# Plain float32 products for the last three down tiles, a final norm without GpSimd, and first low parts from VectorE

## The chip, the cores and the metric

The kernel runs on one core of a Trainium2 chip. The metric is the device time of one execution in microseconds, lower is better. Of the engines, PE is TensorE (matrix products), DVE is VectorE, ACT is ScalarE, POOL is GpSimd and SP is SyncE, which here only issues DMAs.

## The reference, cut to what matters

One encoder layer on 1024 rows of width 1024: attention, mLSTM and a gated MLP side by side, a layer norm, then a mixture of 16 experts in which each expert chooses 128 rows, and a last layer norm. Only the part from the experts on is touched.

```python
def expert_choice_ffn(h, w_router, w_gate, w_up, w_down):
    cap = max(1, min(S, EC_CAPACITY_FACTOR * S // N_EXPERTS))      # 128 rows an expert
    aff = softmax(einsum('bsd,de->bse', h, w_router))
    gate, idx = lax.top_k(aff.transpose(0, 2, 1), cap)
    xg = jax.vmap(lambda hb, ib: hb[ib])(h, idx)
    hid = silu(einsum('becd,edf->becf', xg, w_gate)) * einsum('becd,edf->becf', xg, w_up)
    ye = einsum('becf,efd->becd', hid, w_down) * gate[..., None]
    ...                                                             # scatter-add of ye to the rows

    y = expert_choice_ffn(h2, w_router, w_gate, w_up, w_down)
    return layer_norm(DN_ALPHA * x + (1 + g2) * y, ln_g[1], ln_b[1])
```

Everything is float32; D is 1024, the hidden width F is 2048.

## The kernel before

**Splitting.** PE multiplies float32 here in three products of a shorter format, fp32r: an operand is split in a high part H (ACT copies it to fp32r) and a low part L (the operand minus H, by DVE or POOL), and `mm3` (lines 42 to 44) adds H by H, H by L and L by H. `split` (lines 37 and 38) does it for activations, `part` (lines 1295 and 1296) for weights.

**Tiles.** `experts` walks the weights in 192 tiles of 2 MB, four quarters of F an expert: gate tile g n, up tile u n, and down tile d n-1 for n from 0 to 63. `fetch` loads a tile on SP's queue into one of eight raw buffers, as soon as the four parts of the tile that held it are made. Each tile has four pieces of 128x1024; `part` makes H and L of a piece, in a ring of NP = 5 pairs, five pieces ahead of `product`, which issues six products of 128x512 for it (two column halves, three products each). Down products of an expert add up in one accumulator `ye` of 128x1024 in PSUM.

**An expert's rows.** `pick` (lines 1303 to 1318) makes a one-hot matrix on DVE, multiplies it on PE to the list of chosen rows `ix` and their gates `sw`, and gathers the rows by an indirect DMA on POOL (line 1315) to `xg`; `turn` transposes them on PE and splits them (`xH`, `xL`). `gate` is the silu on ACT, `hidden` the product with the up result on DVE, `turn_hidden` (T, line 1376) the transposes and `parts_hidden` (U) the split of the hidden rows. `finish` scales an expert's result and adds it to the rows in DRAM (`acc_dr`) by an indirect DMA on POOL; all rows there already hold the residual.

**Start.** Ahead of the experts lies `routing`, the choice of rows: a sort on DVE whose steps are the maximum and minimum at lines 1201 and 1202. `experts` is written behind it: eight fetches, the first five parts with their L on POOL, then `pick(0)` and `turn(0)`.

**End.** The order of the last 16 products and of the final norm is written out in the string `LAST`. Each word is an operation with a number: P product, W part, T and U as above, G and H the last `gate` and `hidden`, L row loads to three raw buffers, Q the gather of the last expert's rows from `acc_dr`, y and z that expert's scaled result plus those rows, and then for rows i (eight tiles of 128 rows, and tile 8 for the last expert's 128 chosen rows) the sums by ACT (a) or DVE (d), the root (q), the reciprocal (r), the normalisation (p by ACT), the gain (g by POOL, m by DVE), the shift (s by POOL, h by DVE), or gain and shift in two fused steps on DVE (e, f). Z scatters tile 8 over the output by an indirect DMA on POOL, behind the writes of all others. An engine works off its instructions in the order of this string.

Of the kernel before, what the change touches and what calls it, by code (L numbers as in the profile page):

```python
# [25 lines left out]
class K:  # L26
# [1233 lines left out]
    def experts(self):  # L1260
        nc, tc, a, v, s, g, pe = self.nc, self.tc, self.a, self.v, self.s, self.g, self.pe
        NR, NP = 8, 5
        with tc.tile_pool(name="ew", bufs=1, reuse_waits="tile") as ew, \
# [26 lines left out]
            def part(eng):  # L1290
                t, q = divmod(len(pieces), 4)
                H = ew.tile([128, 1024], F32R, tag="wH", name=f"H{t}_{q}", bufs=NP)
# [92 lines left out]
            for i in range(NP):  # L1385
                part(g)
            for f in (pick, turn):
                for _ in f(0):
                    pass
            nc.scalar.dma_start(g2r, self.bcast_rows(self.mod_dr[3:4, :], 1024))  # L1390
            all_ = 4 * len(tiles)
            for i in range(all_ - 16):
# [161 lines left out]
```

## Time and profile before

| | us |
|---|---|
| median of 3 runs | 1718.21 (1717.98 to 1719.55) |
| the profiled execution | 1719.36 |
| its span, first to last instruction | 1717.6 |
| PE busy in the span | 1590.0 (93%) |
| DVE busy | 1498.6 (87%) |
| ACT busy | 1124.4 (65%) |
| POOL busy | 300.8 (18%) |
| mean granted clock of TensorE | 0.965 |

The shares are means over stages with different limits, so they are read stage by stage: the attention part and routing to 573.57 us, the experts from there to 1648.81 (the start of the last but one hidden tile's transposes, T0), the last 16 pieces to the end of PE at 1676.27, and the rest of the final norm to 1717.57.

### The profile page before, as it was taken

How to read it: one execution, taken by the hardware profiler on the slowest of the kernel's cores; microseconds unless marked ns; L12 is line 12 of the kernel's file. 1: busy time of each engine (PE TensorE's matmuls, PEld its weight loads, DVE VectorE, ACT ScalarE, POOL GpSimd, SP SyncE). 2: the span in 40 equal slices, each digit the busy share in tenths (PEclk: the TensorE clock that was granted, in tenths of full speed). 3: DMA queues.
4: the chain of work that ended last, by engine and by line, in shares of the span. 5: the costliest groups of instructions: out<-in, count | busy, mean ns of one | idle time of the engine just before them, and what ended most of it. 6: DMA issues, size and time to landing. Idle time of an engine off the chain costs nothing.

```text
span 1717.6 us, 22528 instructions
## 1 busy us (share of the span) xinstructions
PE 1590.0 (93%) x8147; PEld 1338.3 (78%) x8147; DVE 1498.6 (87%) x2031; ACT 1124.4 (65%) x1446; POOL 300.8 (18%) x338
## 2 busy tenths in 40 slices
PE   5889999999993799999999999999999999999990
PEld 5678799798883588888888888888888888888870
DVE  6878863597987699999999999999999999999987
ACT  4443433496222478787878787778787878787873
POOL 2514331285115000000000000000000000000045
PEclk9899999999995799999999999999999999999995
DMA  9154631113369499999999999999999999999933
GB/s 341 63 173 154 212 103 31 62 50 113 114 256 341 140 387 380 386 386 376 388 382 379 391 383 388 385 377 389 384 378 390 382 387 385 378 386 386 368 134 121
DMA packets 218823, 498.33 MB, mean 290 GB/s; under 512 B 9420, under 2 KB 31784, under 8 KB 218712
## 3 DMA queue, kind: packets, MB, share of 16 engines
q1 hardware_dynamic: 209680, 467.77, 73.9%
q0 software_dynamic: 5984, 21.60, 4.5%
q10 hardware_dynamic: 3048, 7.52, 1.2%
q8 instruction: 64, 1.05, 0.3%
q14 instruction: 47, 0.39, 0.1%
HBM read 475.79 MB, written 21.07 MB: 289 GB/s over the span
## 4 chain that ended last, share of the span: by engine, by line
PE 83%; DVE 12%; issue 2%; ACT 1%; DMA 1%; POOL 1%; ACTq 0%; SPq 0%; POOLq 0%; DVEq 0%
PE pu L42 7%; PE pg L42 7%; PE pg L44 7%; PE pg L43 7%; PE pu L44 7%; PE pu L43 7%; PE ye L42 7%; PE ye L44 7%; PE ye L43 7%; PE mx L44 2%; PE mx L42 2%; PE mx L43 2%; PE ht L1376 2%; PE tp L42 2%; PE tp L43 1%
## 5 line engine op out<-in xcount | busy, mean ns | idle before, releaser
L1296 DVE TENSOR_TENSOR L<-rd,H 128x1024 fp32r<-128x1024 f32 x251 | 306.5, 1243 | 27.2 <-ACT H L1295 21.4
L1296 DVE TENSOR_TENSOR L<-ru,H 128x1024 fp32r<-128x1024 f32 x253 | 306.5, 1229 | 23.3 <-ACT H L1295 12.8
L1295 ACT ACTIVATE H<-ru 128x1024 fp32r<-128x1024 f32 x256 | 271.9, 1063 | 83.4 <-PE pg L44 61.9
L1295 ACT ACTIVATE H<-rd 128x1024 fp32r<-128x1024 f32 x256 | 271.0, 1059 | 73.8 <-PE pg L44 47.3
L1295 ACT ACTIVATE H<-rg 128x1024 fp32r<-128x1024 f32 x256 | 271.6, 1062 | 63.4 <-PE ye L44 54.6
L1296 DVE TENSOR_TENSOR L<-rg,H 128x1024 fp32r<-128x1024 f32 x252 | 302.3, 1220 | 7.5 <-ACT H L1295 1.6
L42 PE MATMUL pg<-H,xH 128*128 128x512 f32 x512 | 207.4, 405 | 0.0
L44 PE MATMUL pg<-H,xL 128*128 128x512 f32 x512 | 201.1, 393 | 0.0
L42 PE MATMUL pu<-H,xH 128*128 128x512 f32 x512 | 200.6, 392 | 0.0
L43 PE MATMUL pg<-L,xH 128*128 128x512 f32 x512 | 200.5, 392 | 0.0
L44 PE MATMUL pu<-H,xL 128*128 128x512 f32 x512 | 199.2, 389 | 0.0
L43 PE MATMUL pu<-L,xH 128*128 128x512 f32 x512 | 199.2, 389 | 0.0
L43 PE MATMUL ye<-L,hH_h 128*128 128x512 f32 x504 | 196.5, 390 | 1.8 <-POOL L L1296 1.8
L42 PE MATMUL ye<-H,hH_h 128*128 128x512 f32 x504 | 197.6, 392 | 0.0
L44 PE MATMUL ye<-H,hL_h 128*128 128x512 f32 x504 | 196.3, 389 | 0.0
L1315 POOL DMA_INDIRECT xg<-h_dr,ix x16 | 23.9, 1491 | 848.8 <-PE ye L44 724.8
L44 PEld LDWEIGHTS pg<-H,xL 128*128 128x128 f32 x512 | 96.5, 188 | 21.0 <-DVE xL L38 0.2
L44 PEld LDWEIGHTS pu<-H,xL 128*128 128x128 f32 x512 | 96.1, 188 | 20.2
L43 PEld LDWEIGHTS ye<-L,hH_h 128*128 128x128 f32 x504 | 94.7, 188 | 21.8 <-POOL L L1296 2.6
L43 PEld LDWEIGHTS pu<-L,xH 128*128 128x128 f32 x512 | 96.1, 188 | 19.6
L42 PEld LDWEIGHTS pu<-H,xH 128*128 128x128 f32 x512 | 96.1, 188 | 19.6
L43 PEld LDWEIGHTS pg<-L,xH 128*128 128x128 f32 x512 | 97.0, 189 | 17.6
(453 smaller groups left out, 3040.5 us busy)
## 6 DMA issues: line engine op xcount, KB each, us to landing
rg<-in_w_gate_dram SPq DMA_DIRECT2D x64, 2048.0 KB, 9.1
ru<-in_w_up_dram SPq DMA_DIRECT2D x63, 2048.0 KB, 11.8
rd<-in_w_down_dram SPq DMA_DIRECT2D x63, 2048.0 KB, 11.0
B<-in_w_ada_dram SPq DMA_DIRECT2D x64, 256.0 KB, 3.0
B<-in_w_in_dram SPq DMA_DIRECT2D x18, 512.0 KB, 4.9
H<-in_w_ada_dram SPq DMA_DIRECT2D x8, 1024.0 KB, 10.9
B<-in_x_dram SPq DMA_DIRECT2D x4, 1024.0 KB, 5.5
B<-in_w_out_dram SPq DMA_DIRECT2D x8, 512.0 KB, 3.2
```

What stands on the lines that cost most here:

```text
L42: pe.matmul(out, sH, mH, start=first, stop=False)
L43: pe.matmul(out, sH, mL, start=False, stop=False)
L44: pe.matmul(out, sL, mH, start=False, stop=last)
L1295: s.activation(H, src, AF.Copy)
L1296: eng.tensor_tensor(L, src, H.bitcast(F32), ALU.subtract)
L1315: g.indirect_dma_start(out=xg, out_offset=None, in_=self.h2_dr, in_offset=bass.IndirectOffsetOnAxis(ap=ix[:, :1], axis=0))
L1376: pe.transpose(p[:, k, :], state["sg"][:, 128 * k:128 * k + 128], self.idn)
```

## The change

It has five parts.

1. At the start, `pick(0)` comes first; then four parts, with L on DVE; then `turn(0)`; then the fifth part, with L on DVE.
2. The last three down tiles, d61 to d63, are not split: `part` hands out the raw piece, `product` issues two plain float32 products for it in place of six, and the hidden rows of these tiles are one float32 copy by ACT.
3. The fetches of d62 and d63 are taken out of `part` and placed in `LAST` (F) behind the row loads L0, L1 and L2; Q comes directly behind them.
4. In the final norm POOL does nothing but the two indirect DMAs. Row sums are made by ACT (a) or, for row 1 and tile 8, by DVE; then two fused steps on DVE, e: (x - mean) * gain and f: times the reciprocal, plus shift.
5. The last tile's products are ordered by column halves, A12 to A15 for the first half and B12 to B15 for the second, and y, z and the statistics x of tile 8 are steps of half a row.

```diff
+            plain = lambda t: tiles[t][0] == "d" and tiles[t][1] >= 4 * NE - 3
...
             def part(eng):
                 t, q = divmod(len(pieces), 4)
+                if plain(t):
+                    pieces.append((raws[t][:, 1024 * q:1024 * q + 1024], None))
+                    return
...
-                if q == 3 and len(raws) < len(tiles):
+                if q == 3 and len(raws) < len(tiles) - 2:
                     fetch(nc.sync)
...
-            def product(i):
+            def product(i, us=(0, 1)):
...
-                    for u in range(2):
+                    H, L = hid[n]
+                    for u in us:
                         c = slice(512 * u, 512 * u + 512)
+                        if L is None:
+                            pe.matmul(state["acc"][:, c], H[:, q, :], WH[:, c], start=(j + q == 0), stop=(j == 3 and q == 3))
+                            continue
...
+            def parts_hidden(n):
+                if n >= 4 * NE - 3:
+                    H = ew.tile([128, 4, 128], F32, tag=("hH", "hL", "xH")[n - 4 * NE + 3], name=f"h{n}", bufs=1 + (n == 4 * NE - 1))
+                    s.activation(H, state["ht"], AF.Copy)
+                    hid[n] = (H, None)
+                    return
...
-            for i in range(NP):
-                part(g)
-            for f in (pick, turn):
-                for _ in f(0):
-                    pass
+
+            for _ in pick(0):
+                pass
+            for i in range(NP - 1):
+                part(v)
+            for _ in turn(0):
+                pass
+            part(v)
...
+        def sums(i):
             m, x = mv[:, i, :], X[i]
+            s.activation(B[11], x, AF.Identity, accum_out=m[:, 3:4])
+            s.activation(m[:, 0:1], m[:, 3:4], AF.Copy, scale=-1.0 / D)
+            s.activation(B[11], x, AF.Square, bias=m[:, 0:1], accum_out=m[:, 1:2])
...
+        def gain(i):
+            v.scalar_tensor_tensor(X[i], X[i], mv[:, i, 0:1], B[0], op0=ALU.add if byact[i] else ALU.subtract, op1=ALU.mult)
+
+        def shift(i):
+            v.scalar_tensor_tensor(X[i], X[i], mv[:, i, 2:3], B[1], op0=ALU.mult, op1=ALU.add)
             if i < 8:
                 nc.sync.dma_start(a["out"][0, 128 * i:128 * i + 128, :], X[i])
...
+        def scaled(q):
+            c = slice(512 * q, 512 * q + 512)
+            v.scalar_tensor_tensor(X[8][:, c], state["acc"][:, c], state["w"][:, 2:3], g2r[:, c], op0=ALU.mult, op1=ALU.mult)
+
+        def final_sum(q):
+            c = slice(512 * q, 512 * q + 512)
+            v.tensor_tensor(X[8][:, c], X[8][:, c], B[10][:, c], ALU.add)
+
+        def spread(q):
+            v.bn_stats(st8[:, q, :], X[8][:, 512 * q:512 * q + 512])
+            if q:
+                v.bn_aggr(mv[:, 8, 0:2], st8)
...
-    LAST = "T0 P0 P1 P2 W0 W1 W1 P3 U0 P4 W0 G0 P5 P6 W1 L0 L1 P7 W1 L2 W1 H0 W0 P8 P9 W0 W0 T1 U1 W1 P10 P11 P12 P13 d0 d1 W1 P14 q0 r0 q1 d2 r1 d3 p0 P15 p1 a5 y8 d4 q4 d6 Q0 g0 r4 q5 g1 q6 d7 s0 p4 q3 r5 p5 q7 r6 z8 r3 h1 q2 m5 g4 p3 s4 p6 r7 m3 m6 s5 r2 h6 e7 s3 f7 p2 a8 q8 r8 g2 h2 p8 m8 s8 Z0"
+    LAST = "L0 L1 F0 L2 F0 Q0 T0 U0 W0 a0 d1 P0 P1 e0 e1 a2 W0 e2 W0 P2 W0 P3 G0 q0 q1 q2 r0 f0 r1 f1 r2 f2 P4 P5 P6 P7 H0 a3 e3 q3 r3 f3 a4 e4 q4 r4 f4 W0 W0 W0 W0 W0 W0 W0 W0 P8 P9 T1 U1 P10 P11 a5 e5 q5 r5 f5 A12 A13 A14 A15 B12 B13 B14 B15 a6 e6 a7 y0 z0 x0 q6 r6 f6 e7 q7 r7 f7 y1 z1 x1 q8 e8 r8 f8 Z0"
```

How the change moves the instructions shows at three places. The first is DVE's end of the routing and start of the experts; OH and ix are `pick(0)`, xL is `turn(0)`, and L_0 to L_3 are low parts of weight pieces (rg, ru: raw gate and up tile). Before:

```order
L1303 TENSOR_TENSOR OH_5246<-C,late 128x1024 [waits DVE_49]
L1311 COPY sw_5257<-sp_5248 128x6 [waits PE_49]
L1313 TENSOR_TENSOR ix_5259<-sw_5257 128x1 [waits DVE_49]
L1317 TENSOR_TENSOR sw_5257<-sw_5257 128x1
L1318 TENSOR_TENSOR sw_5257<-sw_5257 128x1 [waits DVE_49]
L38 TENSOR_TENSOR xL_5266<-xt_5267,xH_5265 128x512 [waits DMAHW5_49,DMASW2_49,Activation_49]
L38 TENSOR_TENSOR xL_5266<-xt_5274,xH_5265 128x512 [waits Activation_49]
L1296 TENSOR_TENSOR L_1_5290<-ru_5210,H_1_5289 128x1024 [waits DMAHW1_49,Activation_49]
```

And with the change:

```order
L1308 TENSOR_TENSOR OH_5224<-C,late 128x1024 [waits DVE_49]
L1316 COPY sw_5235<-sp_5226 128x6 [waits PE_49]
L1318 TENSOR_TENSOR ix_5237<-sw_5235 128x1 [waits DVE_49]
L1322 TENSOR_TENSOR sw_5235<-sw_5235 128x1
L1323 TENSOR_TENSOR sw_5235<-sw_5235 128x1 [waits DVE_49]
L1301 TENSOR_TENSOR L_0_5244<-rg_5208,H_0_5243 128x1024 [waits DMAHW7_49,Activation_49]
L1301 TENSOR_TENSOR L_1_5248<-rg_5208,H_1_5247 128x1024 [waits Activation_49]
L1301 TENSOR_TENSOR L_2_5252<-rg_5208,H_2_5251 128x1024 [waits Activation_49]
L1301 TENSOR_TENSOR L_3_5256<-rg_5208,H_3_5255 128x1024 [waits Activation_49]
L38 TENSOR_TENSOR xL_5262<-xt_5263,xH_5261 128x512 [waits DMAHW5_49,DMASW2_49,Activation_49]
L38 TENSOR_TENSOR xL_5262<-xt_5270,xH_5261 128x512 [waits Activation_49]
L1301 TENSOR_TENSOR L_0_5278<-ru_5210,H_0_5277 128x1024 [waits DMAHW1_49,Activation_49]
```

The four low parts of the first gate tile and the first of the up tile now stand in DVE's row, around the pair of xL; before, POOL had them ahead of its gather.

The second place is ACT's row at the last gate and up tiles, from the last up tile's first high part (H_0<-ru) on; hH_h and h are copies of the hidden rows, fx the accumulated rows, fmv their statistics. Before:

```order
L1295 ACTIVATE H_0_14648<-ru_14298 128x1024 [waits DMAHW4_49,DVE_49,PE_49]
L1295 ACTIVATE H_1_14652<-ru_14298 128x1024 [waits DVE_49,PE_49]
L1295 ACTIVATE H_2_14656<-ru_14298 128x1024 [waits DVE_49,PE_49]
L37 ACTIVATE hH_h_14666<-ht_14624 128x512
L1295 ACTIVATE H_3_14677<-ru_14298 128x1024 [waits DVE_49,PE_49]
L1367 ACTIVATE sg_14681<-pg_14629 128x512 [waits PE_49]
```

And with the change:

```order
L1388 ACTIVATE h_14611<-ht_14606 128x512 [waits PE_49]
L1300 ACTIVATE H_0_14613<-ru_14298 128x1024 [waits DMAHW4_49,DVE_49]
L1473 ACTIVATE fx_14599,fmv<-fx_14587 128x1024 [waits DMAHW7_49]
L1474 ACTIVATE fmv<-fmv 128x1 [waits Activation_49]
L1475 ACTIVATE fx_14599,fmv<-fx_14587,fmv 128x1024 [waits Activation_49]
L1473 ACTIVATE fx_14599,fmv<-fx_14592 128x1024 [waits DMAHW1_49,Activation_49]
L1474 ACTIVATE fmv<-fmv 128x1 [waits Activation_49]
L1475 ACTIVATE fx_14599,fmv<-fx_14592,fmv 128x1024 [waits Activation_49]
L1300 ACTIVATE H_1_14642<-ru_14298 128x1024 [waits DVE_49,PE_49]
L1300 ACTIVATE H_2_14647<-ru_14298 128x1024 [waits DVE_49,PE_49]
L1300 ACTIVATE H_3_14657<-ru_14298 128x1024 [waits DVE_49,PE_49]
L1374 ACTIVATE sg_14667<-pg_14624 128x512 [waits PE_49]
```

Between H_0 and H_1 of the last up tile now stand the sums of two rows, and H_1 to H_3 follow them.

The third place is the end of DVE's row; fy is tile 8, L1494 (before) and L1501 the scaling of the accumulator ye. Before:

```order
L1478 TENSOR_TENSOR fx_14719<-fx_14719,fx_14699 128x1024 [waits Activation_49]
L1465 RECIPROCAL fmv<-fmv 128x1
L1469 SCALAR_TENSOR_TENSOR fmv<-fmv 128x1 [waits DVE_49]
L1484 TENSOR_TENSOR fx_14719<-fx_14719,fx_14699 128x1024
L1497 SCALAR_TENSOR_TENSOR fx_14719<-fx_14719,fmv,fx_14699 128x1024
L1482 SCALAR_TENSOR_TENSOR fx_14719<-fx_14719,fmv,fx_14699 128x1024 [waits DVE_49]
L1465 RECIPROCAL fmv<-fmv 128x1 [waits Activation_49]
L1467 TENSOR_TENSOR fmv<-fmv 128x1 [waits DVE_49]
L1484 TENSOR_TENSOR fx_14704<-fx_14704,fx_14699 128x1024 [waits Pool_49]
L1478 TENSOR_TENSOR fy<-fy,fx_14699 128x1024 [waits Activation_49]
```

And with the change:

```order
L1501 SCALAR_TENSOR_TENSOR fy<-ye_14447,sw_13712,g2r 128x512 [waits DMASW1_49,PE_49]
L1505 TENSOR_TENSOR fy<-fy,fx_14599 128x512 [waits DMASW2_49,DVE_49]
L1508 BN_STATS fst_14586<-fy 128x6 [waits DVE_49]
L1482 RECIPROCAL fmv<-fmv 128x1 [waits Activation_49]
L1489 SCALAR_TENSOR_TENSOR fx_14599<-fx_14599,fmv,fx_14587 128x1024 [waits DVE_49]
L1486 SCALAR_TENSOR_TENSOR fx_14599<-fx_14599,fmv,fx_14587 128x1024 [waits DMAHW7_49]
L1482 RECIPROCAL fmv<-fmv 128x1 [waits Activation_49]
L1489 SCALAR_TENSOR_TENSOR fx_14599<-fx_14599,fmv,fx_14587 128x1024 [waits DVE_49]
L1501 SCALAR_TENSOR_TENSOR fy<-ye_14447,sw_13712,g2r 128x512
L1505 TENSOR_TENSOR fy<-fy,fx_14599 128x512 [waits DVE_49]
L1508 BN_STATS fst_14586<-fy 128x6 [waits DVE_49]
L1510 BN_AGGR fmv<-fst_14586 128x2 [waits DVE_49]
```

Behind these follow the gain, reciprocal and shift of tile 8. The scaling of ye stands near the end now, in two halves, of which the first names a wait for PE and the second none.

## Rows read from the trace of the kernel before

**Rows 1.** the stages, table by windows; x: instructions
```profile
core 0: us, PE busy (x) PEld busy (x) DVE busy (x) ACT busy (x) POOL busy (x), PEclk, DMA share, GB/s
...
540.66:552.41 11.75, 0.00 (x0) 0.00 (x0) 11.64 (x6) 0.00 (x0) 11.63 (x6) 0.50 1.03 388
...
573.57:1648.81 1075.24, 1075.03 (x5008) 888.17 (x5009) 1014.49 (x997) 857.78 (x909) 57.49 (x30) 1.00 1.02 378
1648.81:1676.27 27.46, 23.89 (x106) 18.51 (x103) 22.05 (x23) 17.00 (x19) 22.14 (x9) 1.00 0.07 19
1676.27:1717.57 41.30, 0.00 (x1) 0.00 (x0) 32.02 (x38) 15.17 (x24) 22.88 (x10) 0.53 0.29 115
```

**Rows 2.** DVE's timeline around the routing's end and the start of the experts: start, us, what
```profile
543.22 2.26 DVE L1201 TENSOR_TENSOR T<-TB 128x64 f32<-128x64 f32 x1
...
552.41 0.23 DVE L1201 TENSOR_TENSOR T<-TB 128x64 f32<-128x64 f32 x1
...
553.60 0.23 DVE L1201 TENSOR_TENSOR TB<-T 128x64 f32<-128x64 f32 x1
...
575.40 1.50 DVE L38 TENSOR_TENSOR xL<-xt,xH 128x512 fp32r<-128x512 f32 x2 [6.80 <-ACT xH L37]
...
602.93 2.36 DVE L1296 TENSOR_TENSOR L<-rg,H 128x1024 fp32r<-128x1024 f32 x2
```

**Rows 3.** POOL's timeline over the same stretch
```profile
540.77 9.23 POOL L1296 TENSOR_TENSOR L<-rg,H 128x1024 fp32r<-128x1024 f32 x4
549.96 2.34 POOL L1296 TENSOR_TENSOR L<-ru,H 128x1024 fp32r<-128x1024 f32 x1
569.18 1.09 POOL L1315 DMA_INDIRECT xg<-h_dr,ix  x1 [16.89 <-issue]
603.51 1.48 POOL L1315 DMA_INDIRECT xg<-h_dr,ix  x1 [33.24 <-PE ye L44]
```

**Rows 4.** PE's timeline where plain float32 products stand among split ones
```profile
316.05 1.88 PE L632 MATMUL sd<-B,WT 128*128 128x512 f32 x4
317.36 0.79 PE L42 MATMUL tp<-H,B 128*128 128x512 f32 x1
318.00 0.39 PE L43 MATMUL tp<-H,B 128*128 128x512 f32 x1
```

**Rows 5.** the chain that ended last, by time, around the first products
```profile
579.20 0.43 PE pg L44
...
580.17 0.23 PE pg L44
```

**Rows 6.** the same chain, transposes of the last but one hidden tile
```profile
1649.04 0.44 PE ht L1376 x4
```

**Rows 7.** PE's timeline in the last products, two of its waits
```profile
1665.94 0.50 PE L43 MATMUL ye<-L,hH_h 128*128 128x512 f32 x1 [1.21 <-POOL L L1296]
...
1670.97 0.50 PE L44 MATMUL ye<-H,xL_h 128*128 128x512 f32 x1 [1.75 <-DVE xL_h L38]
```

**Rows 8.** ACT's timeline at the end: one high part, first and last of a row's sums
```profile
1657.77 1.06 ACT L1295 ACTIVATE H<-rd 128x1024 fp32r<-128x1024 f32 x1 [0.29 <-PE pu L44]
...
1678.89 1.04 ACT L1450 ACTIVATE fx<-fx 128x1024 f32<-128x1024 f32 x1
...
1681.34 0.19 ACT L1452 ACTIVATION_READ_ACCUMULATOR fx<-fx,fmv 128x1 f32 x1
```

**Rows 9.** SP's queue timeline, the loads of the accumulated rows
```profile
1630.57 8.94 SPq L1438 DMA_DIRECT2D fx<-acc_dr  x8
```

**Rows 10.** DVE's timeline, a fused step on half a row and on a whole row
```profile
526.26 0.75 DVE L1077 SCALAR_TENSOR_TENSOR H<-H,mm,B 128x512 f32<-128x512 f32 x1
...
1701.52 1.27 DVE L1497 SCALAR_TENSOR_TENSOR fx<-fx,fmv,fx 128x1024 f32<-128x1024 f32 x1
```

**Rows 11.** POOL's timeline, its last two
```profile
1708.95 2.34 POOL L1484 TENSOR_TENSOR fy<-fy,fx 128x1024 f32<-128x1024 f32 x1 [3.96 <-DVE fy L1478]
1711.57 1.00 POOL L1503 DMA_INDIRECT out_dram<-fy,ix  x1 [0.28 <-POOL fy L1484]
```

More of the change, by code (lines that the diff above doesn't have):

```diff
@@ L1417, in experts @@
             ops = self.final(ew, g2r, state)
-            ops.update({"W": lambda eng: part(g if eng else v), "P": lambda i: product(all_ - 16 + i), "G": lambda _: gate(n),
-                        "H": lambda _: hidden(n), "T": lambda i: turn_hidden(n - 1 + i),
-                        "U": lambda i: parts_hidden(n - 1 + i, *((("hH", "hL"), 1), (("xH", "xL"), 2))[i])})
+            at = lambda i: all_ - 16 + i
+            ops.update({"W": lambda _: part(v), "F": lambda _: fetch(nc.sync), "P": lambda i: product(at(i)),
+                        "A": lambda i: product(at(i), (0,)), "B": lambda i: product(at(i), (1,)), "G": lambda _: gate(n),
+                        "H": lambda _: hidden(n), "T": lambda i: turn_hidden(n - 1 + i), "U": lambda i: parts_hidden(n - 1 + i)})
             for t in self.LAST.split():
@@ L1477, in gain, with stats @@
-        def gain(i, eng):
-            eng.tensor_tensor(X[i], X[i], B[0], ALU.mult)
-        def shift(i, eng):
-            if eng is None:
-                v.scalar_tensor_tensor(X[i], X[i], mv[:, i, 2:3], B[1], op0=ALU.mult, op1=ALU.add)
-            else:
-                eng.tensor_tensor(X[i], X[i], B[1], ALU.add)
+        st8 = ew.tile([128, 2, 6], F32, name="fst8")
+        byact = [f"a{i}" in self.LAST.split() for i in range(9)]
+        def stats(i):
+            st = ew.tile([128, 2, 6], F32, tag="fst", name=f"fst{i}", bufs=2)
+            for q in range(2):
+                v.bn_stats(st[:, q, :], X[i][:, 512 * q:512 * q + 512])
+            v.bn_aggr(mv[:, i, 0:2], st)
@@ L1502, in scatter @@
+        def final_sum(q):
[5 more added lines that the diff above has]
+                v.bn_aggr(mv[:, 8, 0:2], st8)
         def scatter(_):
             g.indirect_dma_start(out=a["out"][0], out_offset=at, in_=X[8], in_offset=None)
-        byact = [f"a{i}" in self.LAST.split() for i in range(9)]
-        return {"L": load, "Q": rows, "d": lambda i: stats(i, False), "a": lambda i: stats(i, True),
-                "q": lambda i: root(i, byact[i]), "r": lambda i: scale(i, byact[i]),
-                "p": lambda i: apply(i, s), "b": lambda i: apply(i, v), "m": lambda i: gain(i, v), "g": lambda i: gain(i, g),
-                "e": fused, "f": lambda i: shift(i, None), "h": lambda i: shift(i, v), "s": lambda i: shift(i, g), "y": scaled, "z": final_sum, "Z": scatter}
@@ L1514 @@
-    LAST = "T0 P0 P1 P2 W0 W1 W1 P3 U0 P4 W0 G0 P5 P6 W1 L0 L1 P7 W1 L2 W1 H0 W0 P8 P9 W0 W0 T1 U1 W1 P10 P11 P12 P13 d0 d1 W1 P14 q0 r0 q1 d2 r1 d3 p0 P15 p1 a5 y8 d4 q4 d6 Q0 g0 r4 q5 g1 q6 d7 s0 p4 q3 r5 p5 q7 r6 z8 r3 h1 q2 m5 g4 p3 s4 p6 r7 m3 m6 s5 r2 h6 e7 s3 f7 p2 a8 q8 r8 g2 h2 p8 m8 s8 Z0"
+        return {"L": load, "Q": rows, "d": stats, "a": sums, "q": root, "r": inverse, "e": gain, "f": shift,
+                "y": scaled, "z": final_sum, "x": spread, "Z": scatter}
+    LAST = "L0 L1 F0 L2 F0 Q0 T0 U0 W0 a0 d1 P0 P1 e0 e1 a2 W0 e2 W0 P2 W0 P3 G0 q0 q1 q2 r0 f0 r1 f1 r2 f2 P4 P5 P6 P7 H0 a3 e3 q3 r3 f3 a4 e4 q4 r4 f4 W0 W0 W0 W0 W0 W0 W0 W0 P8 P9 T1 U1 P10 P11 a5 e5 q5 r5 f5 A12 A13 A14 A15 B12 B13 B14 B15 a6 e6 a7 y0 z0 x0 q6 r6 f6 e7 q7 r7 f7 y1 z1 x1 q8 e8 r8 f8 Z0"
```

39 lines of the change are left out of this document (5 added, 34 removed).

## The prediction

> **What bounds the kernel now.** I read the busy time by stage first [rows 1]. From the first matrix product of expert 0 to the last tile's hidden transposes (573.57 to 1648.81) PE is busy 1075.03 of 1075.24 us at clock 1.00: in that stage only the number and length of PE's instructions count. The other three stages are not like it. In 540.66:552.41 PE does nothing, and six DVE instructions fill 11.64 us; in 1648.81:1676.27 PE is busy 23.89 of 27.46; in 1676.27:1717.57 PE has ended, DVE is busy 32.02 and POOL 22.88 of 41.30. The change touches each of these places and, for one tile, the PE-bound stage. Then I read the timelines of the engines in the short stages, to see what each waits for.
>
> **Part 1, first low parts from POOL to DVE.** The routing sort compares keys on DVE, 128x64 elements at a time. Six such steps stand in the first short stage; the 2.26 us of the one at 543.22 is ten times the 0.23 of the one at 552.41, which has the same line, shape and types. POOL's five subtractions begin at 540.77 and end at 552.30 [rows 2, 3]: DVE slows down and recovers with them. The next six steps run from 552.41 to 553.60 = 1.19 us [rows 2]. So without POOL's work the stage of 11.75 should take 1.19: **-10.56**. The sort is on the chain, since index, gather and expert 0 follow it.
> What DVE takes over has cover: it is idle 6.80 us before xL (575.40), waiting for the gathered rows [rows 2]; four subtractions at 1.18 (2.36 for two [rows 2]) are 4.7, starting at 568.6. If that cover were gone, xL would be late by the part that sticks out. The fifth subtraction comes behind the xL pair and is wanted only four pieces later.
> The gather's issue on POOL now runs beside those subtractions. The issue of the second gather, at 603.51, ran beside DVE's pair at 602.93 and took 1.48, where the first with DVE idle took 1.09 [rows 2, 3]. I take **+0.4**, with 0 as the low end. The high end is that the issue waits for all four: it would start not at 569.18 but at 568.6+4.7 = 573.3, +4.1; I stay near the low end, because the second gather is the same instruction beside the same kind of subtraction. [...]
> One more thing moves: tile 8's fetch is queued on SP when the first tile's four parts are done, about 12 us later; PE needs that tile only after the eight that are already there, 8x4x1.36 = 43 us of products, so nothing.
>
> **Part 2, plain products.** The spatial gating of the first part of the kernel (line 632) already holds plain float32 products of 128x512. From 316.05 to 318.00 lie two of them (their line shows four records, two a product) and one split one [rows 4]. A split product is 0.23 from the next at full clock [rows 5], so two plain ones are 1.95-0.23 = 1.72. A piece of a down tile was six split products, 6x0.23 = 1.36 (unrounded spacing 0.227), and is two plain ones now: +0.36. Tile d61 lies in the PE-bound stage: 4 pieces, **+1.44**. (d62 and d63 are in part 3.) Twelve ACT copies and twelve subtractions go, but ACT and DVE are not what that stage waits for: nothing.
>
> **Part 3, from T0 to PE's end, 27.46 before.** It is transposes, 2x0.44 = 0.88 [rows 6]; sixteen pieces of 1.36 = 21.8; the rest, 4.8, are waits, the longest of them 1.75 for xL_h and 1.21 for a POOL low part [rows 7]. Both kinds go: the last two tiles have no low parts. In their place: 0.88 + 8x1.36 + 8x1.72 = 25.5 of work, and one new wait. ACT works in order, and the new order puts the h62 copy, H_0 of the last up tile and the sums of rows 0 and 2 ahead of H_1 (second order listing). A sum is 2.64 (1678.89 to 1681.53 [rows 8]), an H 1.06 [rows 8], a copy of half a tile an estimated 0.6: counted from T0's start, 0.44+0.1+0.6+1.06+5.28+1.06 = 8.5 for H_1, and PE wants it after T0 and five pieces, at 7.2. PE waits 1.4. L_1 follows 1.2 later, +1.0; behind L_1 DVE has e2 (the gain of row 2, 1.2) before L_2, again +1.0. With 0.3 for the rest 3.7 of waits, so 29.2 to 29.3: **+1.85**. Bounds: 25.5 (no waits, -2.0) and 31 (one more wait like the 1.75).
> SP's queue: the row loads (eight of 0.52 MB) and two constants of that size stand now ahead of the fetches of d62 and d63 (2.1 MB each) instead of behind. Before, they were issued from 1630.57 on, in 8.94 us [rows 9]; with parts 1 and 2 that is 1621.8. All of it, 9.4 MB at the 378 GB/s of the stage [rows 1], is 25 us: there by 1646.7. T0 is then at 1640.1, d62's first product 15 us behind it at 1655, d63's at 1662.5: 8 us of slack and more, so nothing. If that cover is gone, PE waits for what is missing.
>
> **Part 4, behind PE's end, 41.30 before.** DVE had 38 instructions there and POOL ten [rows 1]; POOL's last gain, 2.34 long, ends at 1711.29, its scatter is issued at 1711.57, and the span ends 6.28 behind that gain [rows 11]. Now POOL has only the scatter. What is left for DVE is fixed by the third order listing: the first half step y0 waits for PE, and the second, y1, names no wait of its own. The scheduler keeps the accumulator as one tile, so y0 waits for B15, the last product: **the column halves give no early start**. Behind PE's end then come, on DVE in order: y0 z0 x0, r6 f6, e7, r7 f7, y1 z1 x1, then q8 on ACT, e8 r8 f8. A full gain or shift is 1.27 [rows 10]: five, 6.2 to 6.35 (they start 1.21 apart). Half steps: 0.75 for the fused one [rows 10], no less than 0.6, since half of a 1.27 is 0.64: six, 3.8 to 4.5. Small ones (three reciprocals, the merge of two statistics, a root and its handover) about 1. Sum 11.0 to 11.9, I take 11.5; with the 6.28 unchanged 17.8 to 17.9: **-23.4**. Bounds 16.0 (y0 z0 x0 done while B12 to B15 run, -2) and 20 (ACT's sums of rows 6 and 7, 2x2.64, end late by 2).
>
> **Sum.** -10.56 +0.4 +1.44 +1.85 -23.4 = **-30.3**, from a span of 1717.6 to 1687.3. The profiled execution took 1719.36, 1.76 over its span and 1.15 over the median of 1718.21; so 1687.9, say **1688.0** for the median.
>
> **The rivals.**
> B, *the gather held by DVE*: +4.1 instead of +0.4, so 1691.7. For it: only one row shows a gather beside subtractions, and there were two, not four. Against: that row, 1.48. Chance 0.08.
> C, *the sort is slow for another reason*: the steps stay at 2.3 and 10.2 are missing, 1698. Against: recovery and POOL's end lie 0.1 apart [rows 2, 3]. Chance 0.03.
> D, *TensorE's clock*: at 0.51 of the clock split products stood 0.43 apart at 579.20 and 0.23 at 580.17, once granted [rows 5]; the transposes began the work 6 us before, at 573.57. Each us longer at the lower level (1.2 instead of 2.4 GHz) gives away 0.47. With new waits in the tail, or another start, 2 to 8 us more: 1690 to 1693. Against: 1.00 in rows 1 over both PE stages, the tail's 4.8 of waits among them. Chance 0.10.
> E, *the halves do what they are for* (y0 starts at A15's end): 2 less, 1686. Against: y1 without a wait. Chance 0.05.
> F, *slower*: the clock at the experts' start is not given back for long. To lose the 30.3 and 3.4 more, PE would have to stay at the lower level for 33.7/0.47 = 72 us; from there the kernel is slower, at 1721.6 and above. Against: before, the rise came 6 us behind the first transposes, and the work behind it is the same. Chance 0.02.
> *The change does no good in part 3* (the waits of ACT's order double) is within the range: +3.7, 1691.5.
>
> **How the numbers follow.** The forecast itself has 0.72. Its own bounds: part 1 0 to +4.1 for the gather, part 3 -2 to +1.7, part 4 -2 to +2; taken together some 4 down and 5 up. B, D and E lie in 1684 to 1696; C and F do not, 0.05, and some of D. So the range is **1684 to 1696**. A measurement of this kernel can tell 0.2%, 3.4 us, from no change. Faster by more: 0.96 (all but F and mishaps of more than 27 us); within 0.2%: 0.02; slower: 0.02.
>
> **What would show it.** Part 1: the six sort steps at 0.23 and no POOL work before the gather; gather issue at 1.5 or less; xL not later than its xH. Part 2: the records of the last three down tiles 0.43 apart. Part 3: two waits of about 1 to 1.4 of the last up tile's products for H_1, L_1 and L_2, none for weights. Part 4: y0 starting behind the last product, DVE without gaps for 11.5, then 6.3. Wrong would be: a wait of PE for d62 or d63, a clock below 1.00 between T0 and PE's end, POOL's gather starting only when DVE's fourth subtraction ends.

## The result and the profile after

The changed kernel takes 1688.33 us (median of 4 runs, 1686.48 to 1690.56) against 1718.1 (4 runs, 1716.14 to 1719.55): a ratio of 0.9828, 95% interval 0.9811 to 0.9845. The forecast was 1688.0, in a range of 1684 to 1696. The profiled execution took 1690.56, with a span of 1688.7.

The table by windows of the changed kernel, cut at the same events as [rows 1]: the start of the sort steps, expert 0's transposes, T0, PE's end, the end. Columns are as there.

```profile
core 0: us, PE busy (x) PEld busy (x) DVE busy (x) ACT busy (x) POOL busy (x), PEclk, DMA share, GB/s
542.64:543.83 1.19, 0.00 (x0) 0.00 (x0) 1.09 (x6) 0.00 (x0) 0.15 (x1) 0.50 1.06 404
542.64:565.50 22.86, 3.29 (x27) 2.42 (x27) 17.02 (x64) 0.00 (x0) 1.66 (x2) 0.50 0.58 214
565.50:1641.37 1075.87, 1075.66 (x5000) 885.90 (x5001) 1011.96 (x994) 854.59 (x906) 58.23 (x31) 1.00 1.02 378
1641.37:1671.17 29.80, 28.01 (x89) 16.49 (x87) 23.28 (x27) 26.27 (x51) 0.00 (x0) 0.94 0.44 175
1671.17:1688.70 17.53, 0.01 (x1) 0.00 (x0) 10.94 (x15) 0.29 (x1) 0.98 (x1) 0.63 0.22 90
```

The first six sort steps take 1.19 instead of 11.75. Against [rows 1] the stages are:

| stage | before | after | measured | forecast |
|---|---|---|---|---|
| ahead of the sort steps | 540.66 | 542.64 | +1.98 | 0 |
| sort steps to expert 0's transposes | 32.91 | 22.86 | -10.05 | -10.16 |
| transposes to T0 | 1075.24 | 1075.87 | +0.63 | +1.44 |
| T0 to PE's end | 27.46 | 29.80 | +2.34 | +1.85 |
| PE's end to the end | 41.30 | 17.53 | -23.77 | -23.4 |
| span | 1717.6 | 1688.7 | -28.9 | -30.3 |

The first row is no effect of the change: that code is the same, and in the eleven runs below, which hold it unaltered (one of them the changed kernel once more, at 541.0), the stage took from 537.7 to 541.2. It is what makes single executions differ by some us; so below, stages of one trace are compared with stages of another, and whole times only where there are several runs.

DVE's timeline where part 1 of the change stands (start, us, what), of the changed kernel: two of the sort steps, the four low parts, xL.

```profile
542.79 0.21 DVE L1202 TENSOR_TENSOR TB<-T 128x64 f32<-128x64 f32 x1
543.04 0.22 DVE L1201 TENSOR_TENSOR T<-TB 128x64 f32<-128x64 f32 x1
...
559.93 4.63 DVE L1301 TENSOR_TENSOR L<-rg,H 128x1024 fp32r<-128x1024 f32 x4
567.34 0.69 DVE L38 TENSOR_TENSOR xL<-xt,xH 128x512 fp32r<-128x512 f32 x1 [2.77 <-ACT xH L37]
```

The steps are at 0.21 to 0.23, as [rows 2] has them once POOL had ended. The low parts fill 4.63 of DVE's wait, and 2.77 of it are left before xL, which still waits for ACT.

POOL's and PE's timelines of the changed kernel, one answer each: the first expert's gather; the scatter of tile 8; the products of d61, and the products around the waits in the last up tile.

```profile
560.60 1.51 POOL L1320 DMA_INDIRECT xg<-h_dr,ix  x1 [17.80 <-issue]
```

```profile
1682.75 0.98 POOL L1513 DMA_INDIRECT out_dram<-fy,ix  x1 [51.72 <-DVE fy L1489]
```

```profile
1634.51 7.03 PE L1361 MATMUL ye<-rd,h 128*128 128x512 f32 x16
1641.37 0.60 PE L1383 MATMUL ht<-C,sg 128*128 128x128 f32 x4
...
1648.42 0.39 PE L44 MATMUL pu<-H,xL 128*128 128x512 f32 x1
1649.79 0.49 PE L42 MATMUL pu<-H,xH 128*128 128x512 f32 x1 [0.98 <-ACT H L1300]
1651.05 0.50 PE L43 MATMUL pu<-L,xH 128*128 128x512 f32 x1 [0.77 <-DVE L L1301]
...
1652.70 0.63 PE L42 MATMUL pu<-H,xH 128*128 128x512 f32 x1
1653.38 0.79 PE L43 MATMUL pu<-L,xH 128*128 128x512 f32 x1
```

The gather's issue takes 1.51, where [rows 3] has 1.09 for the same one. The eight plain products of d61 (sixteen records) run from 1634.51 to the transposes at 1641.37: 6.86, or 1.715 a piece.

### The profile page after: what moved, and what is told of

It reads as the page before. It is cut to its first block, busy times and chain, and to the rows that moved or that the text cites. A ratio compares the mean times of both kernels' runs of the same rounds, so it can differ in the third digit from the quotient of the medians.

```text
span 1688.7 us, 22428 instructions
## 1 busy us (share of the span) xinstructions
PE 1594.1 (94%) x8123; PEld 1334.0 (79%) x8123; DVE 1470.4 (87%) x2015; ACT 1115.2 (66%) x1451; POOL 246.1 (15%) x317
## 4 chain that ended last, share of the span: by engine, by line
PE 85%; DVE 9%; issue 2%; ACT 2%; DMA 1%; POOL 1%; ACTq 0%; POOLq 0%; SPq 0%; DVEq 0%
PE pu L42 7%; PE pu L43 7%; PE pu L44 7%; PE pg L42 7%; PE pg L44 7%; PE pg L43 7%; PE ye L44 7%; PE ye L42 7%; PE ye L43 7%; PE mx L44 2%; PE mx L42 2%; PE mx L43 2%; PE ht L1383 2%; PE tp L42 2%; PE tp L44 1%
## 5 line engine op out<-in xcount | busy, mean ns | idle before, releaser
L1301 DVE TENSOR_TENSOR L<-rd,H 128x1024 fp32r<-128x1024 f32 x244 | 292.8, 1221 | 26.4 <-ACT H L1300 20.9
L1301 DVE TENSOR_TENSOR L<-rg,H 128x1024 fp32r<-128x1024 f32 x256 | 307.0, 1221 | 8.5 <-ACT H L1300 2.7
L1300 ACT ACTIVATE H<-rd 128x1024 fp32r<-128x1024 f32 x244 | 258.6, 1060 | 70.1 <-PE pg L44 47.2
L42 PE MATMUL ye<-H,hH_h 128*128 128x512 f32 x488 | 191.2, 392 | 0.0
L44 PE MATMUL ye<-H,hL_h 128*128 128x512 f32 x488 | 190.0, 389 | 0.0
L43 PE MATMUL ye<-L,hH_h 128*128 128x512 f32 x488 | 190.0, 389 | 0.0
L42 PEld LDWEIGHTS pg<-H,xH 128*128 128x128 f32 x512 | 96.6, 189 | 17.4 <-ACT xH L37 0.3
## 6 DMA issues: line engine op xcount, KB each, us to landing
rd<-in_w_down_dram SPq DMA_DIRECT2D x63, 2048.0 KB, 11.2
```

The source lines that it names most:

```text
L42: pe.matmul(out, sH, mH, start=first, stop=False)
L43: pe.matmul(out, sH, mL, start=False, stop=False)
L44: pe.matmul(out, sL, mH, start=False, stop=last)
L1300: s.activation(H, src, AF.Copy)
L1301: eng.tensor_tensor(L, src, H.bitcast(F32), ALU.subtract)
```

## The experiments

All but the last two alter the changed kernel; of these two, one is the changed kernel again and one alters the kernel before.

**Parts ahead of the pick.** Part 1 of the change undone.

```diff
-            for _ in pick(0):
-                pass
-            for i in range(NP - 1):
-                part(v)
-            for _ in turn(0):
-                pass
-            part(v)
+            for i in range(NP):
+                part(g)
+            for f in (pick, turn):
+                for _ in f(0):
+                    pass
```

> The changed kernel with its start undone: the first five low parts by POOL, written ahead of the first pick, as before. Theory (POOL's subtractions slow the sort on DVE): the sort steps beside them take 2.2 to 2.4 us again, the stretch from the first 128x64 sort step to expert 0's transposes is 32.9 us instead of 22.9, and the kernel takes 1698, 10 more than the changed one. Rival (the sort is slow for another reason): steps at 0.22 and 1688. Rival (the gain of the start is eaten later, by fetches or by the clock): the stretch is longer by 10, but the total by under 5.

1697.6 (1695.57 to 1704.12, 4 runs). DVE's timeline of this kernel, sort steps:

```profile
537.88 2.38 DVE L1202 TENSOR_TENSOR TB<-T 128x64 f32<-128x64 f32 x1
540.29 2.27 DVE L1201 TENSOR_TENSOR T<-TB 128x64 f32<-128x64 f32 x1
...
549.48 0.23 DVE L1201 TENSOR_TENSOR T<-TB 128x64 f32<-128x64 f32 x1
```

POOL's timeline, its fifth subtraction:

```profile
547.02 2.34 POOL L1301 TENSOR_TENSOR L<-ru,H 128x1024 fp32r<-128x1024 f32 x1
```

The steps are slow again and recover where POOL's fifth subtraction ends (547.02 + 2.34 = 549.36). The stretch to the transposes is 32.73, 9.87 more than in the changed kernel. The total is 9.3 more by the medians, and from the sort to the end the two traces differ by 10.0: nothing of the gain was given back further on. The gather's issue is at 1.08 again, so the 0.4 that it costs beside the subtractions is real as well.

**Which work of POOL slows DVE.** Two kernels put extra work of POOL at the place of the old subtractions: ten fills, or ten copies, that nothing reads.

```diff
+            scratch = [ew.tile([128, 1024], F32, tag="wL", name=f"scratch{i}", bufs=NP) for i in range(NP)]
+            for i in range(2 * NP):
+                g.memset(scratch[i % NP], 0.0)
```

> The changed kernel with ten fills of 128x1024 by POOL into the ring of low parts, ahead of the first pick, at the place where the five subtractions stood before; they are extra work that nothing reads. If any work of POOL slows DVE's two-operand sort steps, those beside the fills take over 1 us each. If only POOL instructions that read do, they take 0.22 and the stretch from the first sort step to the transposes is 22.8 as in the changed kernel.

In the other, the last line is `g.tensor_copy(scratch[i % NP], raws[0][:, 1024 * (i % 4):1024 * (i % 4) + 1024])`.

> As the run with fills, but ten copies of 128x1024 from a raw weight tile to the ring, by POOL: one operand read, as against two in a subtraction. If reading is what slows DVE, the sort steps beside the copies take 1 to 1.2 us, the length of one copy, and the stretch grows by several us. If it takes two read operands, the steps stay at 0.22.

One execution each: 1695.01 with the fills, 1697.77 with the copies. DVE's and POOL's timelines with the fills, which POOL ran from 540.62 to 549.60, 0.90 each:

```profile
540.93 0.23 DVE L1201 TENSOR_TENSOR T<-TB 128x64 f32<-128x64 f32 x1
541.08 0.22 DVE L1202 TENSOR_TENSOR T<-TB 128x64 f32<-128x64 f32 x1
...
543.31 6.37 DVE L1214 COPY T<-TB 32x128 f32<-32x128 f32 x1
549.69 0.22 DVE L1215 COPY T<-TB 32x128 f32<-32x128 f32 x1
```

```profile
540.62 8.98 POOL L1400 MEMSET scratch<- 128x1024 f32 x10
```

And beside the copies, from 541.27 to 551.15, 0.99 each:

```profile
541.33 1.06 DVE L1202 TENSOR_TENSOR TB<-T 128x64 f32<-128x64 f32 x1
542.42 0.95 DVE L1201 TENSOR_TENSOR T<-TB 128x64 f32<-128x64 f32 x1
```

Beside fills the two-operand steps keep their 0.22; beside copies each takes as long as one copy, beside subtractions as long as one subtraction. One read operand on POOL's side is enough, and these steps take turns with POOL's work, one instruction each; the stretch to the transposes grew to 30.58. The expectation for the fills failed in another way: the stretch is 28.90 and not 22.8, because a one-operand copy of DVE (0.21 long in the changed kernel) stood for 6.37 until the last of the queued fills had ended. Three of the ten fills were over when it started, and it got no turn between the seven that were left. The Trainium skill's page "SBUF — State Buffer" (section "SBUF: two separate sides") has the first half of this: an operation with two SBUF inputs on VectorE locks out, and is locked out by, only a GpSimd operation that reads SBUF, while a fast-mode one does so with any. These rows agree with it; that the fast-mode one can lose its turn to seven instructions in a row it does not say.

**DVE's copies at the gather.** Four copies by DVE while POOL issues the gather.

```diff
+            scratch = ew.tile([128, 1024], F32, tag="wL", name="scratch", bufs=NP)
+            for i in range(4):
+                v.tensor_copy(scratch, raws[0][:, 1024 * i:1024 * i + 1024])
             for i in range(NP - 1):
                 part(v)
```

> The changed kernel with four extra float32 copies of 128x1024 by DVE from the first raw tile to a spare ring tile, behind the index and ahead of the four low parts, so that they run when POOL issues the first gather; nothing reads them. By the rule of the Trainium skill (page SBUF - State Buffer, section SBUF: two separate sides) the issue on POOL waits for DVE's copies: it starts or ends only behind them, 2 us or more late. By the rows so far (issue 1.09 with DVE idle, 1.51 beside subtractions) it takes 1.1 to 1.6 and starts 0.85 behind the index.

One execution, 1686.32. DVE's, POOL's and PE's timelines of this kernel:

```profile
555.91 0.16 DVE L1318 TENSOR_TENSOR ix<-sw 128x1 int32<-128x1 f32 x1
...
556.26 2.98 DVE L1402 COPY scratch<-rg 128x1024 f32<-128x1024 f32 x4
559.15 4.63 DVE L1301 TENSOR_TENSOR L<-rg,H 128x1024 fp32r<-128x1024 f32 x4
```

```profile
556.92 1.08 POOL L1320 DMA_INDIRECT xg<-h_dr,ix  x1 [17.80 <-issue]
```

```profile
561.23 1.97 PE L1336 MATMUL xt<-C,xg 128*128 128x128 f32 x8 [5.55 <-DMA xg<-h_dr,ix]
```

The issue starts 0.85 behind the index, as in the changed kernel and in the one before, and ends in the midst of the copies, in 1.08: less than the 1.51 beside subtractions. The rows do not land late either: the transposes that wait for them start 4.31 behind the issue's start, against 4.39 in the kernel before, where DVE was idle, and 4.90 in the changed kernel. The rule that the expectation names, by which GpSimd cannot write the descriptors of its DMA during such a copy of VectorE (the Trainium skill, page "SBUF — State Buffer", section "SBUF: two separate sides"), is not borne out by this run. Rival B, which was about subtractions, falls by the 1.51 of the changed kernel itself.

**The last three tiles split again.** d61 to d63 with high and low parts, in the changed kernel's order, parts five pieces ahead.

```diff
-            plain = lambda t: tiles[t][0] == "d" and tiles[t][1] >= 4 * NE - 3
+            plain = lambda t: False
...
-... P2 W0 P3 G0 q0 ... f2 P4 P5 P6 P7 H0 ... f4 W0 W0 W0 W0 W0 W0 W0 W0 P8 P9 T1 U1 P10 P11 ...
+... P2 W0 P3 W0 G0 q0 ... f2 P4 W0 P5 W0 P6 W0 P7 W0 H0 ... f4 P8 W0 P9 W0 T1 U1 P10 W0 P11 ...
```

> The changed kernel with d61 to d63 split again: high parts by ACT, low parts by DVE, six products a piece, hidden rows with low parts; the parts of d62 and d63 are made five pieces ahead. If only PE's own length counts, it is 12 x 0.36 = 4.3 us faster than the changed kernel (1684). If what the plain products save is work of DVE and ACT in the tail (eight subtractions of 1.15, two more for hidden rows, eight copies of 1.06 in a stage where DVE has 4 us of idle), PE waits for low parts: the stretch from T0 to PE's end grows from 29.8 to 33 or more, and the kernel takes 1690 to 1695.

1694.8 (1691.93 to 1695.57, 4 runs), 6.5 slower than the changed kernel. The table by windows from T0 to PE's end and from there to the end, a second one of the first half of this stretch, and PE's timeline there, five of its waits:

```profile
1637.09:1675.63 38.54, 28.42 (x105) 21.17 (x103) 34.87 (x39) 33.85 (x59) 0.00 (x0) 0.87 0.37 149
1675.63:1693.20 17.57, 0.00 (x1) 0.00 (x0) 10.94 (x15) 0.29 (x1) 0.99 (x1) 0.60 0.22 90
```

```profile
1637.09:1650.00 12.91, 10.50 (x46) 7.89 (x45) 11.48 (x13) 12.11 (x18) 0.00 (x0) 1.00 0.50 199
1650.00:1655.00 5.00, 3.47 (x16) 2.53 (x14) 4.89 (x8) 4.99 (x9) 0.00 (x0) 1.00 0.28 111
```

```profile
1645.51 0.50 PE L42 MATMUL pu<-H,xH 128*128 128x512 f32 x1 [0.98 <-ACT H L1300]
1646.77 0.50 PE L43 MATMUL pu<-L,xH 128*128 128x512 f32 x1 [0.76 <-DVE L L1301]
...
1656.69 0.50 PE L43 MATMUL ye<-L,hH_h 128*128 128x512 f32 x1 [3.21 <-DVE L L1301]
1660.69 1.12 PE L1383 MATMUL ht<-C,sg 128*128 128x128 f32 x4 [2.58 <-DVE sg L1378]
...
1668.74 0.64 PE L44 MATMUL ye<-H,xL_h 128*128 128x512 f32 x1 [1.92 <-DVE xL_h L38]
```

DVE is busy 34.87 of 38.54: it has become the bound, and PE waits for it three times over 1 us, part of it at a clock of 0.50. The stage is 8.7 longer, against 1.8 shorter in the stage before it; the last stage, 17.57, is as long as in the changed kernel. So, in this order of the tail, the plain products cost PE time and pay by what they take from DVE, where the final norm needs it; that is the second of the two cases that the expectation names. All low parts are DVE's here. The kernel before left some of the last ones to POOL, and that was not tried in the new order.

These rows also show something about TensorE's clock: PE has the two waits in the last up tile here too (0.98 and 0.76), among the same products, and the clock stays at 1.00 until 1655. It is below 1.00 only later, behind the wait of 3.21.

**Two accumulators.** The column halves in a tile each.

```diff
-                        state["acc"] = ps.tile([128, 1024], F32, tag="ye", name=f"ye{e}", bufs=1)
+                        state["acc"] = [ps.tile([128, 512], F32, tag=f"ye{u}", name=f"ye{u}_{e}", bufs=1) for u in range(2)]
...
```

> The changed kernel with the accumulator as two tiles of 128x512, one for each column half (the earlier experts' scaling is then two half instructions). Theory (the halves give no early start because y0 waits for the last product of the whole tile): y0 now starts behind A15, about 3 us before PE's end, DVE's 3 us of waiting go, and PE's end to the kernel's end is 14.6 instead of 17.5: 1685.5. Rival (DVE's chain is held by ACT's sums of rows 6 and 7 anyway): y0 early, but the reciprocal of row 6 waits, and 1 us or less is gained.

1685.13 (1683.31 to 1685.63, 4 runs), as expected. The end of DVE's timeline in the changed kernel, y0, y1 and the last step:

```profile
1671.22 0.75 DVE L1501 SCALAR_TENSOR_TENSOR fy<-ye,sw,g2r 128x512 f32<-128x512 f32 x1 [2.97 <-PE ye L1361]
...
1677.31 0.75 DVE L1501 SCALAR_TENSOR_TENSOR fy<-ye,sw,g2r 128x512 f32<-128x512 f32 x1
...
1681.19 1.28 DVE L1489 SCALAR_TENSOR_TENSOR fy<-fy,fmv,fx 128x1024 f32<-128x1024 f32 x1
```

And y0 with two accumulators, where PE ends at 1668.91, with the table by windows from there to the end:

```profile
1665.90 0.74 DVE L1503 SCALAR_TENSOR_TENSOR fy<-ye,sw,g2r 128x512 f32<-128x512 f32 x1
```

```profile
1668.91:1683.40 14.49, 0.00 (x1) 0.00 (x0) 8.02 (x11) 0.29 (x1) 0.99 (x1) 0.65 0.27 109
```

In the changed kernel y0 waits 2.97 for the last product; with a tile for each half it starts 3.0 ahead of it, without a wait, and the last stage is 14.49 instead of 17.53. The halves had been cut in the instructions, but not in the tile on which the wait rests.

**Parts before sums.** In `LAST`, the last up tile's parts ahead of the sums of rows 0 and 2.

```diff
-... T0 U0 W0 a0 d1 P0 P1 e0 e1 a2 W0 e2 W0 P2 W0 P3 G0 ...
+... T0 U0 W0 d1 P0 W0 P1 W0 P2 W0 P3 a0 e0 e1 a2 e2 G0 ...
```

> The changed kernel with the four parts of the last up tile ahead of the sums of rows 0 and 2, in ACT's and DVE's order; all else as it was. Theory (PE's waits in the last up tile come from ACT working in order, and the fall of TensorE's clock behind them comes from these waits): no wait of PE for H or L there, granted clock 1.00 from T0 to PE's end, that stretch 25.9 instead of 29.8; ACT's sums end no earlier, so a part may come back behind PE's end: 1684 to 1686. Rival (the clock falls there for another reason, such as the plain products): the stretch is 27.5 with some us at 0.5.

1689.87 (1687.19 to 1690.66, 4 runs): no gain. The table by windows from T0 to PE's end, and the one wait left in PE's timeline:

```profile
1638.76:1667.81 29.05, 25.90 (x89) 15.64 (x87) 23.37 (x27) 26.39 (x51) 0.00 (x0) 1.00 0.43 171
```

```profile
1656.85 0.66 PE L1383 MATMUL ht<-C,sg 128*128 128x128 f32 x4 [3.15 <-DVE sg L1378]
```

PE's work is 25.90 at a clock of 1.00: the waits for H and L and the fall of the clock are gone, as the theory said. That these waits bring the fall by themselves is not shown by it: in the run with d61 to d63 split again, waits of the same length did not. But the shifts of rows 0 to 2, now later, stood ahead of the hidden product H0 in DVE's order, and T1 waited 3.15 for it: the wait had moved.

**Hidden product earlier.** The same, with H0 ahead of those shifts.

```diff
-... G0 q0 q1 q2 r0 f0 r1 f1 r2 f2 P4 P5 P6 P7 H0 a3 ...
+... G0 P4 P5 P6 P7 H0 q0 q1 q2 r0 f0 r1 f1 r2 f2 a3 ...
```

> The run with parts before sums, and in it the last tile's hidden product (H0) ahead of the reciprocals and shifts of rows 0 to 2 in DVE's order. Theory (PE's wait of 3.15 for sg there came from DVE working in order, with three shifts ahead of H0): T1 waits for nothing, T0 to PE's end is 25.9 with the granted clock at 1.00. DVE's sum of work up to y0 is the same, so y0 now waits for DVE's own row steps and not for PE: PE's end to the end is 18.5 to 19, and T0 to the end about 44.6 instead of 46.6. Rival (the clock or another wait takes it back): T0 to the end 46 or more.

One execution, 1685.98. T0 to PE's end is 26.93 and the rest 17.58, 44.5 in all, as expected (44.6), but not in its parts (25.9, and 18.5 to 19). T1 waits for nothing; ACT's copy of the last hidden rows stands behind two row sums instead, and PE waits 0.98 for it. y0 still waits for PE, 0.48, and not for DVE's own row steps as expected: DVE's work is now nearly as long as PE's.

**The tail reordered.** From these: two accumulators, the row work that needs no product put into the idle time of ACT and DVE ahead of T0, what PE needs put first.

```diff
...
-L0 L1 F0 L2 F0 Q0 T0 U0 W0 a0 d1 P0 P1 e0 e1 a2 W0 e2 W0 P2 W0 P3 G0 q0 q1 q2 r0 f0 r1 f1 r2 f2 P4 P5 P6 P7 H0 a3 e3 q3 r3 f3 a4 e4 q4 r4 f4 ... P8 P9 T1 U1 P10 P11 a5 e5 q5 r5 f5 A12 ... B15 a6 e6 a7 y0 z0 x0 q6 r6 f6 e7 q7 r7 f7 ...
+L0 L1 F0 L2 F0 Q0 a0 d1 a2 d3 e1 e3 T0 U0 W0 P0 W0 P1 W0 P2 W0 P3 G0 q0 q1 q2 q3 e0 e2 r0 f0 P4 P5 P6 P7 H0 a4 q4 r1 f1 r2 f2 r3 f3 e4 r4 f4 ... P8 P9 T1 U1 P10 P11 a5 q5 a6 q6 a7 q7 e5 r5 f5 A12 ... B15 e6 y0 z0 x0 r6 f6 e7 r7 f7 ...
```

> The changed kernel with the accumulator in two tiles and a new order of the end: sums of rows 0 and 2 on ACT and statistics and gains of rows 1 and 3 on DVE ahead of T0 (both engines idle there for 6 to 7 us), the parts of the last up tile ahead of the other row steps, the hidden product ahead of three of the four first shifts, ACT's sums of rows 5 to 7 behind the last hidden copy. If the three measured pieces add up (no waits of PE and no fall of its clock, -3.9; y0 behind A15; DVE's work moved into its idle time), T0 to the end is 40 to 42 us against 47.3 in the changed kernel and 44.3 with two accumulators: 1681 to 1683. Rival (DVE in order meets a wait on ACT's sums of rows 5 to 7, or the clock falls): 44 or more, 1685.

1680.73 (1678.57 to 1683.14, 5 runs), a ratio of 0.9782 to before (0.9769 to 0.9796). Its table by windows from T0 on:

```profile
1639.96:1665.64 25.68, 25.68 (x89) 15.73 (x87) 23.79 (x29) 19.07 (x36) 0.00 (x0) 1.00 0.51 201
1665.64:1680.20 14.56, 0.01 (x1) 0.00 (x0) 8.06 (x11) 0.29 (x1) 0.99 (x1) 0.60 0.27 108
```

PE waits for nothing from T0 to its end, at full clock; 40.24 in all, in the range expected for this stretch (the total is 0.3 below its range). What bounds it now is DVE, whose chain behind PE's end is 8.3, and the 6.3 of the scatter.

**The changed kernel again**, for that comparison.

> The changed kernel again, on the chip of the run with the reordered tail, to compare them: 1688, T0 to the end 47.3, and a fall of the clock for about 3.5 us behind the waits of the last up tile. If that fall was a chance of one execution, the clock is 1.00 there and the stretch from T0 to PE's end is 28.2.

1687.92 (1687.1 to 1689.69, 5 runs), 0.9826 to before (0.9813 to 0.984): the reordered kernel is 7.2 faster, and the intervals are apart. The clock falls as it did the first time. Both traces, by windows around the waits of the last up tile, first the first:

```profile
1648.80:1651.80 3.00, 1.25 (x5) 0.85 (x5) 2.03 (x2) 3.00 (x4) 0.00 (x0) 1.00 0.02 5
1651.80:1655.30 3.50, 3.45 (x9) 2.21 (x9) 3.46 (x5) 3.45 (x8) 0.00 (x0) 0.51 0.00 0
1655.30:1671.17 15.87, 15.87 (x44) 7.55 (x42) 12.77 (x16) 13.19 (x29) 0.00 (x0) 1.00 0.50 199
```

```profile
1649.90:1653.40 3.50, 3.50 (x9) 2.27 (x9) 3.46 (x5) 3.45 (x8) 0.00 (x0) 0.52 0.00 0
```

**Before, without POOL in the row steps.** The kernel before, with its nine gains and shifts of POOL made by DVE at the same places (g to m and s to h in `LAST`).

> The kernel before with one thing altered: the nine gains and shifts that POOL made in the final norm are DVE's, at the same places of the order. DVE gets nine steps of 1.2 = 10.8 us more. If the collision with POOL is what made that stage long (tiny DVE steps of 2.2 instead of 0.15, seven of them, and two long ones), DVE's other work there shrinks by about 17, and PE's end to the end is 30 to 36 instead of 41.3. If it is simply the amount of work left behind PE's end, the stage grows to 45 or more.

One execution, 1715.57. PE ends at 1677.33; the table by windows from T0 to there and from there to the end, and one of the small steps:

```profile
1648.35:1677.33 28.98, 25.34 (x105) 19.63 (x103) 22.75 (x26) 19.18 (x22) 21.19 (x8) 0.94 0.06 19
1677.33:1713.80 36.47, 0.00 (x1) 0.00 (x0) 28.95 (x43) 12.98 (x23) 0.99 (x1) 0.56 0.32 130
```

```profile
1686.88 0.16 DVE L1469 SCALAR_TENSOR_TENSOR fmv<-fmv 128x1 f32<-128x1 f32 x1
```

The small steps are short and nothing runs on POOL, yet the stage is 36.5: 4.8 less than the 41.3 of [rows 1], just outside the range of the theory; DVE's other work shrank by 13.9 (32.02+10.8-28.95), not by 17. So the collision is at most a fifth of the 23.8 that the change took from this stage, net of the work that DVE took over; PE's end also came 1.5 later in this trace, and from T0 to the end it is only 3.3 shorter. The other 19 are for the most part work that is no longer in this stage: in the changed kernel DVE is busy 10.94 behind PE's end instead of 28.95. ACT makes most of the sums, gain and shift are two fused steps, and most of the rows are made before PE has ended; no run separates these three. That DVE is freed of the last low parts does not shorten this stage itself: with them back on DVE it was 17.57, and the stage ahead grew.

The 1.5 are TensorE's clock, at 0.50 for some 3.4 us: its mean is 0.94 from T0 to PE's end, where [rows 1] have 1.00, although PE's products there are the same and its waits too (0.64, 1.22 and 1.78 here, 0.61, 1.21 and 1.75 before).

## Why the prediction was right, and where its terms were not

*Part 1* held as it was put: the steps at 0.22, the stretch -10.05 against -10.16, the same when undone (+9.87). The term for the gather, +0.4, was measured as 1.51-1.09 = +0.42; the cover (6.80 idle) was enough. Rival B falls by the gather's 1.51 beside the four subtractions, rival C by the undone start.

*Part 2* held: 1.715 a piece against 1.72. The stage shows +0.63 only, since the granted clock rose earlier: the first product at the higher level started 4.5 us behind the first transposes and not 6.2 as before. Between traces with the same delay the term is there: 1076.77 with the tail reordered (6.2) against 1075.31 before (up to the T0 transposes themselves), +1.46; 1075.51 with parts before sums (3.6) against 1074.04 with the tiles split (3.6), +1.47.

*Part 3* was right in sum, +2.34 against +1.85, but not in its terms, and that the sum came out so near is in part luck. Three waits were forecast at 1.4, 1.0 and 1.0. From start to start, less the 0.23 between products that follow at once, the first two measured 1649.79-1648.42-0.23 = 1.14 and 1651.05-1649.79-0.23 = 1.03 (the 0.98 and 0.77 in the rows count only from the end of the product before), the third 0.25 (1653.38-1652.70, less 0.43 at the lower clock). So the third wait was put four times too high. The rest is what rival D had named: TensorE's clock fell to its lower level (0.51, 1.2 GHz) for 3.5 us behind them. At 0.47 a us that is 1.6. With the 25.68 that the same work took without a wait in the tail reordered, these make 29.7 of the 29.80. I had it against D that the clock stayed up over the longer waits of the tail before; that was one trace, and with the same waits the last run has 0.94 there. A clock below 1.00 there stood among the things that would be wrong, and it came. D's place was right and its price (2 to 8 us) too high, and the smaller waits made up for it. The reading that ACT's order makes these waits is shown by the run with parts before sums; that the waits make the clock fall is not. d62 and d63 were never waited for.

*Part 4* held: 17.53 against 17.8 to 17.9, y0 behind the last product, DVE without a gap for 11.2. That the halves give no early start because the accumulator is one tile is shown by the two accumulators, which gain the 3 us. The bound for that case (-2) was too small: all 2.97 of DVE's idle time could be used.

*The sum* was 1.4 lower than the profiled span, and the stage ahead of the sort, which the change doesn't touch, was 2.0 longer in that execution, the slowest of the four; the four stages that it does touch came to -30.9 against -30.3. That is why the median lies nearer to the forecast than the trace does.

## What to carry to other kernels

Look for the place where an engine that costs nothing by its share (POOL at 18%) runs beside another's critical chain of small instructions: the price was not POOL's time but a turn of 2.3 us for each DVE step of 0.2. It was 10 us at the sort; in the final norm it was the smaller part, and most of the gain there came from less work behind PE's end. In a tail, order each engine's work by what waits for it, and move what needs nothing from the bound engine ahead of it; after each such move look for the next wait, because the engines here worked in the order of their instructions, and a wait tended to move to whatever stood behind (3.15 at T1 once the first two were gone, then 0.98). Cutting instructions in halves buys an early start only if the tile that carries the wait is cut too.

## What the runs showed of the hardware that I had not expected

- A DVE copy of one operand waited 6.37 us behind the seven POOL fills that were left of ten, while two-operand DVE steps ran beside the same fills at 0.22. Beside POOL copies the two-operand steps took 1.0 each; no one-operand step of DVE fell beside these.
- An indirect DMA's issue on POOL took 1.08 beside DVE copies of some 0.7 each, and 1.51 beside DVE subtractions.
- TensorE's clock fell to 0.51 for 3.5 us some 2 us behind the first of two waits of 0.98 and 0.77 in the last up tile, in both traces of the changed kernel and in five other runs with the same waits there. In the run with the three tiles split again the same two waits brought no fall. The kernel before and its variant without POOL in the row steps differ likewise: with the same products and waits up to 1.8 one trace stays at 1.00 and the other has 0.50 for some 3.4 us. And one wait of 3.15, in the run with parts before sums, brought no fall. So the lengths of the waits alone do not decide it; what does stays open. The rise behind the first transposes came 3.6 to 6.2 us after them, in kernels with the same code there.
